# A hybrid pool, DeltaNet and latent-attention block: instruction order from a different scheduling model

## The chip, the cores and the metric

The kernel runs on one core of one Trainium2 chip. Times are device microseconds of one launch. The kernel before has a median of 1241.43 us over three runs (1240.97 to 1242.66). Its profiled execution took 1246.92 us, 5.5 us above that median, of which 1245.1 us is the span from the first to the last instruction.

## The reference

One block over 1024 tokens of width 1024, in float32. All three mixers read one projection of the normed input, and an MLP follows:

```python
h = rms_norm(x, attn_norm[l])
proj = h @ w_in[l]
xa, qkv, z, b, a, c_q, c_kv, k_pe = jnp.split(proj, offsets, axis=-1)
y_a = pool_mixer(xa, ...); y_b = gated_deltanet(qkv, z, b, a, ...); y_c = mla_attention(c_q, c_kv, k_pe, ...)
x = x + jnp.concatenate([y_a, y_b, y_c], axis=-1) @ w_out[l]
h = rms_norm(x, mlp_norm[l])
x = x + jnp.square(jax.nn.relu(h @ w_up[l])) @ w_down[l]
```

The part that matters here is the DeltaNet recurrence. For each of 4 heads a 128 x 128 state passes through the tokens in chunks (64 in the reference, 128 in the kernel), each step of which needs the state of the step before:

```python
v_new = u_i - w_i @ state
o = qd_i @ state + at_i @ v_new
state = state * gl_i + kd_i.T @ v_new
```

## The kernel before

Matrix products in float32 are made of three matmuls on split operands (`mm3`, lines 122 to 125, and `prod`, line 1164 on). A projection tile of 128 columns (`proj_tile`, line 479) is two halves of 512 tokens, and each half is 24 such matmuls into one PSUM bank of tag `mm`. There are 18 tiles: keys, gates, queries, values and the pool mixer.

The stages, in the order of time of the profile:

- 0 to 31 us: loads, norm and transposes of x, then the small projection group (`group`).
- 31 to 168 us: key projections, convolution and SiLU on VectorE and ScalarE (`conv_silu`), key products (line 558), and the latents of attention (`latents`), a queue of generator steps that `pump` advances after each half tile.
- 168 to 222.5 us: `lanes` (line 576 on), the inverses of 32 small triangles, on VectorE, from a DRAM copy of the key products. Their result returns through DRAM (`t_dram`) and feeds `levels` (line 714 on), small 64-row matmuls at line 751.
- 222.5 to 415 us: `chain(h)` for the four heads, 8 chunks each. A chunk is a closed circle between TensorE and VectorE: lines 793 and 794 (state times keys and queries), 796 on VectorE, 801, 805 on VectorE, 810, 815 on VectorE, and then 793 of the next chunk:

```python
PE.matmul(pks[:, 0:P], kt[:, cs_], st, start=True, stop=True)
V.scalar_tensor_tensor(rr, pks[:, 0:P], neg_eg[:, c, h:h + 1], vs[:, c, :], op0=ALU.mult, op1=ALU.add)
PE.matmul(pv_[:, 0:P], tt2[:, c, :], rr, start=True, stop=True)
V.tensor_scalar(vd, pv_[:, 0:P], kd[:, h, c:c + 1], None, op0=ALU.mult)
PE.matmul(pss[:, 0:P], kk[:, c, :], vd, start=True, stop=True)
V.scalar_tensor_tensor(ns, st, el[:, c, h:h + 1], pss[:, 0:P], op0=ALU.mult, op1=ALU.add)
```

  After each four chunks the outputs are normed on VectorE (lines 828 to 832) and transposed on TensorE (line 836). Queries, values, gates and mixer tiles are projected in the same stretch, with `side.append(chain(h))` and `pump` deciding in the source how many chain steps follow each half tile.
- 415 to 530 us: attention (`scores`, `piece`, `weighted`).
- 530 to 720 us: the output product (`out_tile`, with `mm3`), the second norm (`stats`, `spread` with line 1138), and the first MLP products.
- 720 us to the end: the MLP in Strassen-like products (lines 1168 and 1402).

What sets the order on each engine is the framework. The source is traced in program order; a scheduler then simulates the program with a timing model and lets each engine issue what that model says is ready, in order of priority, which follows the program order (`tc.high_priority` lifts `lanes`, and `tc.manual_schedule` keeps the first SyncE loads as written). The list that comes out is fixed: at run time every engine executes its own list in that order, and an instruction that waits holds back all that stand behind it on its engine.

## Time and profile before

| | |
|---|---|
| median of three runs | 1241.43 us |
| profiled execution | 1246.92 us, span 1245.1 us |
| TensorE busy | 1177.1 us, 95% |
| VectorE busy | 858.9 us, 69% |
| ScalarE busy | 570.5 us, 46% |
| GpSimd busy | 292.1 us, 23% |
| chain that ended last | TensorE 72%, VectorE 12%, GpSimd 4%, DMA 4%, ScalarE 4%, issue 3% |

Busy time counts an instruction from its start to its modelled end. TensorE's matmuls overlap each other, so a stretch in which it is always busy isn't a stretch at its peak rate; what such a stretch lacks is idle time. The granted clock is given as a share of full speed: 1.00 is 2.4 GHz and 0.50 is 1.2 GHz.

### The profile page before, as it was taken

The numbers are of one execution on the slowest core, as the hardware profiler recorded it, in microseconds if no ns is written. First come the engines' busy times: TensorE is split into PE (matmuls) and PEld (weight loads), VectorE is DVE, ScalarE is ACT, GpSimd is POOL, SyncE is SP. The second block draws the span as 40 slices with busy tenths as digits, with TensorE's granted clock in tenths as the row PEclk, the third lists the DMA queues.
The fourth block names the chain that finished last, engine by engine and source line by source line (L and its number), as shares of the span: only waits on it lengthen the run. The fifth ranks groups of instructions, "written<-read, shape, count | busy, mean of one in ns | idle before, by whom it ended". The sixth has DMA issues, their size and how long they took to land.

```text
span 1245.1 us, 16313 instructions
## 1 busy us (share of the span) xinstructions
PE 1177.1 (95%) x5802; PEld 966.1 (78%) x5802; DVE 858.9 (69%) x1547; ACT 570.5 (46%) x1187; POOL 292.1 (23%) x327
## 2 busy tenths in 40 slices
PE   6999997899999879998999999999999999999998
PEld 5967775688777658786887788888888888888887
DVE  7576659576576548833688776676659897786863
ACT  6554531455353448722355454555554433333330
POOL 0135542110111285424304334243220000000000
PEclk9999999798999969998999999999999999999999
DMA  7202331211101130184123434433469964442202
GB/s 255 66 19 75 132 104 57 48 50 29 35 14 45 57 106 18 35 330 161 43 77 135 169 144 161 161 144 144 159 228 341 372 220 158 152 136 101 94 26 101
DMA packets 85697, 152.61 MB, mean 123 GB/s; under 512 B 25456, under 2 KB 28656, under 8 KB 85616
## 3 DMA queue, kind: packets, MB, share of 16 engines
q1 hardware_dynamic: 76624, 144.23, 32.9%
q10 hardware_dynamic: 8992, 7.34, 1.9%
q8 instruction: 46, 0.75, 0.2%
q14 instruction: 35, 0.29, 0.1%
HBM read 105.41 MB, written 46.14 MB: 122 GB/s over the span
## 4 chain that ended last, share of the span: by engine, by line
PE 72%; DVE 12%; POOL 4%; DMA 4%; ACT 4%; issue 3%; SPq 0%; POOLq 0%; DVEq 0%; ACTq 0%
PE mm L1402 14%; PE mm L1168 12%; PE sm L1168 6%; PE ch L1402 5%; PE sm L1402 5%; PE mm L125 4%; PE mm L124 4%; PE mm L123 4%; PE ch L1168 3%; DMA upr<-in_w_up_dram 2%; PE sm L751 2%; PE ch L125 1%; DVE tl L588 1%; PE ch L123 1%; PE ch L124 1%
## 5 line engine op out<-in xcount | busy, mean ns | idle before, releaser
L1402 PE MATMUL mm<-dop,dop 128*128 128x512 f32 x768 | 176.0, 389 | 0.0
L1402 PEld LDWEIGHTS mm<-dop,dop 128*128 128x128 f32 x768 | 144.1, 188 | 29.9
L1168 PE MATMUL mm<-H,wop 128*128 128x512 f32 x576 | 139.2, 394 | 3.0 <-DVE uo L1233 3.0
L1168 PEld LDWEIGHTS mm<-H,wop 128*128 128x128 f32 x576 | 108.9, 190 | 27.1 <-DVE uo L1233 4.0
L115 ACT CAST dop<-wdr 128x1024 fp32r<-128x1024 f32 x48 | 50.4, 1050 | 152.5 <-PE mm L1402 62.9
L123 PE MATMUL mm<-H,w 128*128 128x512 f32 x280 | 116.3, 415 | 0.2 <-DVE zs L710 0.2
L125 PE MATMUL mm<-H,w 128*128 128x512 f32 x280 | 115.2, 411 | 0.0
L124 PE MATMUL mm<-H,w 128*128 128x512 f32 x280 | 114.3, 408 | 0.0
L1168 PE MATMUL sm<-op,wop 128*128 128x512 f32 x384 | 92.4, 389 | 1.4 <-ACT p L1231 1.4
L116 POOL TENSOR_TENSOR w<-raw,w 128x1024 fp32r<-128x1024 f32 x15 | 36.5, 2433 | 221.9 <-ACT w L115 191.7
L1168 PEld LDWEIGHTS sm<-op,wop 128*128 128x128 f32 x384 | 72.0, 188 | 16.8 <-ACT p L1231 1.9
L116 DVE TENSOR_TENSOR dop<-wdr,dop 128x1024 fp32r<-128x1024 f32 x48 | 58.6, 1221 | 31.1 <-ACT dop L115 31.1
L1255 ACT ACTIVATE uo<-uo 128x512 f32<-128x512 f32 x48 | 30.3, 631 | 96.9 <-DVE uo L1233 57.0
L116 DVE TENSOR_TENSOR wop<-s,wop 128x512 fp32r<-128x512 f32 x64 | 44.1, 704 | 38.4 <-ACT wop L115 38.4
L1402 PE MATMUL sm<-dop,dop 128*128 128x512 f32 x288 | 67.4, 389 | 0.0
L1402 PE MATMUL ch<-dop,dop 128*128 128x512 f32 x288 | 67.4, 389 | 0.0
L116 DVE TENSOR_TENSOR dop<-H,dop 128x1024 fp32r<-128x1024 f32 x52 | 63.2, 1215 | 0.0
L1402 PEld LDWEIGHTS ch<-dop,dop 128*128 128x128 f32 x288 | 54.1, 188 | 11.2
L1402 PEld LDWEIGHTS sm<-dop,dop 128*128 128x128 f32 x288 | 54.0, 188 | 11.2
L502 DVE SCALAR_TENSOR_TENSOR t2k<-mm,cw,t2k 128x511 f32<-128x511 f32 (+2 forms) x72 | 53.4, 742 | 11.7 <-ACT t2k L499 11.4
L1205 POOL TENSOR_TENSOR s<-upr 128x512 f32<-128x512 f32 x16 | 24.1, 1504 | 159.2 <-DVE uo L1194 73.5
L125 PEld LDWEIGHTS mm<-H,w 128*128 128x128 f32 x280 | 54.0, 193 | 9.1
(395 smaller groups left out, 2684.5 us busy)
## 6 DMA issues: line engine op xcount, KB each, us to landing
H<-u_dram SPq DMA_DIRECT2D x52, 512.0 KB, 4.3
upr<-in_w_up_dram SPq DMA_DIRECT2D x38, 512.0 KB, 4.0
u_dram<-t SPq DMA_DIRECT2D x64, 256.0 KB, 2.0
wdr<-in_w_down_dram SPq DMA_DIRECT2D x32, 512.0 KB, 7.7
u_dram<-uo SPq DMA_DIRECT2D x48, 256.0 KB, 2.1
raw<-in_w_tiles_dram SPq DMA_DIRECT2D x18, 512.0 KB, 3.5
wor<-in_w_out_dram SPq DMA_DIRECT2D x10, 512.0 KB, 8.9
x<-in_x_dram SPq DMA_DIRECT2D x8, 512.0 KB, 3.5
```

Of the source, the lines that this page charges most:

```text
L115: A.copy(hi, src)
L116: (eng or V).tensor_tensor(lo, src, f32(hi), op=ALU.subtract)
L123: PE.matmul(o, ah, bh, start=first, stop=False)
L124: PE.matmul(o, ah, bl, start=False, stop=False)
L125: PE.matmul(o, al, bh, start=False, stop=last)
L502: V.scalar_tensor_tensor(acc[:, s:], pm[:, :512 - s], w, acc[:, s:], op0=ALU.mult, op1=ALU.add)
L588: V.tensor_tensor(TL[:, j + 1:32, 0:m], TL[:, j + 1:32, 0:m], tv, op=ALU.subtract)
L751: PE.matmul(pa[:, c, :], lhs[:, c, :], rhs[:, c, :], start=True, stop=True)
L1168: PE.matmul(o, x_, y_, start=(first and j == 0 and q == 0), stop=(j == 3 and q == 2), skip_group_check=True)
L1205: G.tensor_tensor(v.s12[:, 0], a21, a22, op=ALU.add)
L1255: A.activation(o, o, AF.Relu)
L1402: PE.matmul(o, x_[:, cs_], y_, start=(q in (0, 1, 3) and i == 0 and e == 0), stop=(i == GP - 1 and e == 2), skip_group_check=True)
```

## The change

One argument of the framework's context is set, so that its scheduler takes the timeline simulator for its timing model in place of the default one. The instructions, their sizes, the tiles and the number of buffers are the same; only the order on the engines (and the waits that this order needs) is another.

```diff
-    with tile.TileContext(nc) as tc:
+    with tile.TileContext(nc, schedule_with_timeline_sim=True) as tc:
         block_kernel(tc, *args, o)
```

The order moves on all engines, most of all in the stretch of the key projections and the four chains. On TensorE, in the circle of the second head (`ch` is the PSUM bank of the chain, `mm` that of a projection, `st`, `rr`, `vd` and `vh` what VectorE and ScalarE make between the chain's matmuls), before:

```order
L793 MATMUL ch_600_3166<-st_597_3159,kt_146_982 128x128
L794 MATMUL ch_600_3166<-st_597_3159,qt_369_2294 128x128
L123 MATMUL mm_680_3448<-H_3_99,w_630_3251 128x512
L124 MATMUL mm_680_3448<-H_5_101,w_630_3251 128x512
L125 MATMUL mm_680_3448<-H_3_99,w_631_3252 128x512
L801 MATMUL ch_603_3173<-rr_601_3169,tt2_412_2446 128x128
L123 MATMUL mm_680_3448<-H_3_99,w_630_3251 128x512
L124 MATMUL mm_680_3448<-H_5_101,w_630_3251 128x512
L125 MATMUL mm_680_3448<-H_3_99,w_631_3252 128x512
L810 MATMUL ch_606_3179<-vd_605_3176,ktok_409_2433 128x128
L817 MATMUL ch_608_3183<-vh_604_3175,E_81_691 128x128
L123 MATMUL mm_680_3448<-H_3_99,w_630_3251 128x512
```

and now:

```order
L793 MATMUL ch_600_3166<-st_597_3159,kt_146_982 128x128
L794 MATMUL ch_600_3166<-st_597_3159,qt_369_2294 128x128
L801 MATMUL ch_603_3173<-rr_601_3169,tt2_412_2446 128x128
L810 MATMUL ch_606_3179<-vd_605_3176,ktok_409_2433 128x128
L817 MATMUL ch_608_3183<-vh_604_3175,E_81_691 128x128
L793 MATMUL ch_610_3188<-st_607_3181,kt_146_982 128x128
L794 MATMUL ch_610_3188<-st_607_3181,qt_369_2294 128x128
```

The projection matmuls (lines 123 to 125) that stood two or three between each two steps of the circle stand elsewhere; the steps follow each other directly.

On TensorE at the end of that head and the start of the next (line 836 transposes the normed output `lv`; line 801 is the next head's first chunk), before, with 14 projection matmuls of `mm_718` in the row, of which the first two are shown:

```order
L817 MATMUL ch_615_3199<-vh_614_3197,E_81_691 128x128
L123 MATMUL mm_718_3593<-H_2_98,w_678_3444 128x512
L124 MATMUL mm_718_3593<-H_4_100,w_678_3444 128x512
...
L836 MATMUL ch_642_3340<-ident_79,lv_569_3053 128x128
L801 MATMUL ch_650_3383<-vs_581_3077,tt2_550_2975 128x128
L836 MATMUL ch_642_3340<-ident_79,lv_569_3053 128x128 x3
L125 MATMUL mm_718_3593<-H_2_98,w_679_3445 128x512
```

and now:

```order
L801 MATMUL ch_613_3195<-rr_611_3191,tt2_412_2446 128x128
L817 MATMUL ch_615_3199<-vh_614_3197,E_81_691 128x128
L836 MATMUL ch_642_3340<-ident_79,lv_569_3053 128x128
L801 MATMUL ch_650_3383<-vs_581_3077,tt2_550_2975 128x128
L836 MATMUL ch_642_3340<-ident_79,lv_569_3053 128x128 x3
L810 MATMUL ch_653_3389<-vd_652_3386,ktok_547_2962 128x128
L817 MATMUL ch_655_3393<-vh_651_3385,E_86_704 128x128
L123 MATMUL mm_792_3945<-H_2_98,w_784_3894 128x512
```

The transposes of line 836 now follow the head's last chain matmul at once, and the rest of the next head's first chunk follows them; the projection in that place was issued earlier.

On TensorE at the second norm (line 1138 spreads the norm's factors over the partitions; `mm_1158` and `mm_1160` are tiles of the output product), before:

```order
L124 MATMUL mm_1158_5874<-y_982_4718,H_1124_5562 128x512
L125 MATMUL mm_1158_5874<-y_982_4718,H_1124_5562 128x512
L123 MATMUL mm_1158_5874<-y_506_2818,H_1124_5562 128x512
L1138 MATMUL ch_1154_5851<-dg_1153_5849,ones_86 128x512
L1138 MATMUL ch_1154_5851<-dg_1153_5849,ones_86 128x512
L124 MATMUL mm_1158_5874<-y_506_2818,H_1124_5562 128x512
L125 MATMUL mm_1158_5874<-y_506_2818,H_1124_5562 128x512
L123 MATMUL mm_1158_5874<-y_644_3347,H_1124_5562 128x512
```

and now:

```order
L123 MATMUL mm_1160_5916<-y_961_4625,H_1124_5562 128x512
L124 MATMUL mm_1160_5916<-y_961_4625,H_1124_5562 128x512
L125 MATMUL mm_1160_5916<-y_961_4625,H_1124_5562 128x512
L123 MATMUL mm_1160_5916<-y_982_4718,H_1124_5562 128x512
L124 MATMUL mm_1160_5916<-y_982_4718,H_1124_5562 128x512
L1138 MATMUL ch_1154_5851<-dg_1153_5849,ones_86 128x512
L125 MATMUL mm_1160_5916<-y_982_4718,H_1124_5562 128x512
L123 MATMUL mm_1160_5916<-y_506_2818,H_1124_5562 128x512
```

The product of line 1138 stands 22 output matmuls later: 17 of `mm_1158` and 5 of `mm_1160` went ahead of it.

## Rows read from the trace of the kernel before

**Rows 1.** Span and mean granted TensorE clock of the core.

```profile
core 0: 1245.1 us, clock 0.971
```

**Rows 2.** Busy time by stage: columns as the first row names them, last three clock, DMA.

```profile
core 0: us, PE busy (x) PEld busy (x) DVE busy (x) ACT busy (x) POOL busy (x), PEclk, DMA share, GB/s
31.00:168.00 137.00, 132.65 (x665) 109.21 (x663) 90.67 (x275) 70.09 (x210) 50.55 (x94) 1.00 0.22 72
168.00:222.50 54.50, 39.73 (x176) 32.31 (x177) 42.12 (x99) 9.74 (x15) 21.04 (x32) 0.91 0.29 97
222.50:415.00 192.50, 183.14 (x1175) 148.69 (x1175) 124.30 (x377) 89.39 (x295) 23.03 (x17) 0.93 0.12 30
415.00:470.00 55.00, 43.37 (x212) 33.05 (x213) 28.52 (x48) 28.38 (x65) 32.37 (x39) 0.78 0.30 102
530.00:600.00 70.00, 63.97 (x281) 51.91 (x280) 30.52 (x52) 22.17 (x34) 24.48 (x18) 0.95 0.62 220
720.00:1245.10 525.10, 521.45 (x2301) 431.46 (x2299) 379.12 (x417) 222.87 (x314) 66.70 (x41) 1.00 0.47 168
```

**Rows 3.** Who TensorE waited for: total us, times, longest us.

```profile
...
PE sm L751 <- DMA lv<-t_dram: 13.9, 1, 13.9
...
PE ch L1138 <- DVE dg L1136: 5.8, 1, 5.8
PE s L926 <- ACT H L937: 4.9, 1, 4.9
...
PE ch L836 <- DVE lv L832: 3.7, 2, 2.3
PE ch L836 <- DMA lv<-t_dram: 3.0, 1, 3.0
```

**Rows 4.** Timeline of one chunk: start, us, engine, line, operation, tiles, [idle before].

```profile
...
319.07 0.39 PE L793 MATMUL ch<-st,kt 128*128 128x128 f32 x2
...
319.44 0.47 PE L123 MATMUL mm<-H,w 128*128 128x512 f32 x1
...
319.72 0.35 DVE L796 SCALAR_TENSOR_TENSOR rr<-ch,neg_eg,vs 128x128 f32<-128x128 f32 x1 [0.61 <-PE ch L794]
319.75 0.39 PE L124 MATMUL mm<-H,w 128*128 128x512 f32 x1
...
319.98 0.40 PE L125 MATMUL mm<-H,w 128*128 128x512 f32 x1
...
320.22 0.40 PE L801 MATMUL ch<-rr,tt 128*128 128x128 f32 x2
...
320.65 0.35 DVE L805 TENSOR_SCALAR vd<-ch,kd 128x128 f32<-128x128 f32 x1 [0.58 <-PE ch L801]
...
321.15 0.46 PE L810 MATMUL ch<-vd,ktok 128*128 128x128 f32 x2
...
322.16 0.39 PE L793 MATMUL ch<-st,kt 128*128 128x128 f32 x2
```

**Rows 5.** Timeline at the end of a head, the last one.

```profile
...
410.97 0.49 PE L817 MATMUL ch<-vh,E 128*128 128x128 f32 x2
...
414.68 0.88 DVE L832 TENSOR_SCALAR lv<-lv,sr 128x128 f32<-128x128 f32 x4
...
415.02 0.72 PE L836 MATMUL ch<-ident,lv 128*128 128x128 f32 x3
```

**Rows 6.** Stretches with the lower granted clock (column PEclk).

```profile
213.00:233.40 20.40, 10.44 (x73) 9.32 (x74) 11.07 (x26) 5.53 (x11) 0.00 (x0) 0.50 0.35 88
294.90:305.10 10.20, 10.20 (x58) 8.68 (x58) 4.19 (x11) 4.50 (x18) 0.00 (x0) 0.50 0.10 38
438.30:458.70 20.40, 12.87 (x36) 9.07 (x37) 6.49 (x12) 7.97 (x20) 20.19 (x28) 0.50 0.28 94
```

**Rows 7.** Timeline, TensorE: fourth head's first key transposes and its last key products.

```profile
146.85 0.60 PE L520 MATMUL sm<-ident,kt 128*128 128x128 f32 x4
...
164.03 1.16 PE L558 MATMUL sm<-kt 128*128 128x128 f32 x8
```

## The prediction

> **What bounds the kernel now.** I read the span and the clock first: 1245.1 us at a mean granted clock of 0.971 [rows 1]. Then busy time by stage, to see where TensorE is the limit. From 720 us on it is busy for 521.45 of 525.1 us: nothing can be won there by order, and its list in that part is nearly the old one. In the chains' stage (222.5 to 415) it is busy for 183.14 of 192.5 us at a clock of 0.93, so the stage has 9.36 us idle. In 168 to 222.5 it idles 14.8 us, in 415 to 470 11.6 us at a clock of 0.78 [rows 2]. Then who TensorE waited for: one wait of 13.9 us at line 751 for the inverses from DRAM, 5.8 at line 1138, 4.9 at line 926, 6.7 in three waits at line 836 [rows 3]. So the kernel is bound by TensorE's work, with a few single waits, and the question of this change is where an order puts the independent matmuls (projections) that fill the waits of the dependent ones.
>
> What one chunk of a chain costs shows in the timeline [rows 4]. Line 793 starts at 319.07, line 801 at 320.22, line 810 at 321.15, the next 793 at 322.16: steps of 1.15, 0.93 and 1.01 us, 3.09 together. The steps hold three, three and two projection matmuls (the order of before shows this chunk), which follow each other every 0.23 us (319.75 to 319.98): 8 x 0.23 = 1.86 us. The rest, 3.09 - 1.86 = 1.2 us, is TensorE's own share of the chunk. VectorE's three operations each wait for the matmul before them and are waited for by the next (line 796 starts 0.61 us after its last predecessor on VectorE and waits for 794; line 805 likewise for 801). The circle is one of latency, and the projections ride in it free.
>
> **The change, part by part.** It adds and removes no operation, so every cost is a filler that is gone or a wait that is filled. All sums are made against the profiled 1246.92 us, which is 5.5 us above the median of 1241.43; the difference found is then put on the median.
>
> (a) Bare steps. In the four heads there are 87 steps between dependent matmuls (793 to 801, 801 to 810, 810 to 793). In the list before, none is without something else between; in the list now 42 are bare, in four stretches: the second half of the first head into the second, the second half of the second (its piece is shown), the second half of the third, and nearly all of the fourth. The fillers stand in clumps instead: 13 steps with 13 or more projections hold 237 of them, where before 7 such steps held 132. A clump is longer than the step it covers, so the surplus covers nothing. A bare step keeps its latency, and TensorE idles for the 1.86 / 3 = 0.62 us that fillers took: 42 x 0.6 = +25 us. Bounds: if a step shrinks by one interval of 0.23 us, since the returning matmul no longer stands behind a filler, 42 x 0.39 = +16; if it keeps all of it, 42 x 0.62 = +26. I take +25, by the latencies of the row, because VectorE's two waits show no slack in it.
>
> (b) The norm at the end of four chunks. Line 817 starts at 410.97; the transposes of the normed output (line 836) can start when line 832 has made it, at 415.02 [rows 5]: 4.05 us, of which 0.23 is line 817's own issue, so 3.8 us of idling where nothing stands between. Now 836 follows 817 directly in six of the eight places (one is shown), and the first 801 of the next head's chain stands behind it, so the next chain can't cover it. One of the six has some small products ahead of it, about 2 us by their count. 6 x 3.8 - 2 = 21, less the 6.7 us that TensorE already waits there [rows 3] = +14. Low bound +7: if three of the six are late already for another reason, 3 x 3.8 + 2.3 - 6.7. High bound +14, as all idle time is counted.
>
> (c) The clock. It fell to 0.50 after the long wait (213.0 to 233.4: busy 10.44 of 20.40 us), and from 438.3 to 458.7, where TensorE was busy 12.87 of 20.40; it was also at 0.50 from 294.9 to 305.1 although busy for all of it [rows 6]. So thin work goes with the lower level, and the level can last some 10 us into full work. A bare chunk is busy 1.2 of 3.09 us, thinner than either of the first two. Bounds: 0, if it stays at the present mean of 0.93; above, 14 bare chunks (42 / 3) with 1.1 us more each at half rate = 15.6, and behind each of four stretches 10.2 us at half rate, which lose 5.1 each, 20.4; less what the stage already loses, 0.07 x 192.5 = 13.5: +22.5. The nearest rows lie on both sides, and I take +8, somewhat below the middle, since the bare stretches are short.
>
> The Trainium skill, in "TensorE: Matmul & The Clock Gate", Part 1, section "What's actually happening", says that throttled is the default and that activity releases it. By that alone the clumps behind each stretch would run at the full level, and (c) would be 15.6 - 13.5 = +2; the stretch at 294.9, busy throughout and still at 0.50, speaks against so quick a release, and by it (c) is +22.5. The trace agrees with the rule only in that thin work came with the lower level.
>
> (d) 31 to 168 us. Projections are drawn ahead here: the fourth head's key transposes and products (line 520 at 146.85 to line 558 at 164.03, about 18.3 us with the last product [rows 7]) held 45 projection matmuls, 45 x 0.23 = 10.4 us, that are now issued earlier, so this dependent tail runs almost bare. Line 558 feeds `lanes` through DRAM, and `lanes` feeds the 13.9 us wait; the same seven tile halves as before stand ahead of line 751. What is late here is late there. Bounds: the stage's whole idle time, 137.0 - 132.65 = 4.35 us, won [rows 2]; 10.4 lost. I take +4, nearer to the loss, since the products start after the fillers.
>
> (e) Line 1138. 22 output matmuls, 22 x 0.23 = 5.1 us, now go ahead of it, so its wait of 5.8 us is filled: -5. Bounds: -6.0, all the idle time of 530 to 600 (70 - 63.97 us [rows 2]), and 0 if the second norm's consumers, which start 5 us later, are late instead.
>
> (f) 415 to 470. The first score blocks move up into the fourth chain, ahead of the mixer tile's 24 matmuls (5.6 us), which can now lie where line 926 waited 4.9 us. Bounds: -11.6, all idle of the stage, and +3. I take -3, because line 926 still waits for ScalarE's H.
>
> (g) The other queues. SyncE issues the late weights in another order at 900 to 1000 us, and some output matmuls move into attention's tail. I cost these at nothing: TensorE's row after 720 is full, and that work hides them. If a weight came late the cover would be gone, with a loss of its lateness; the stage's DMA share of 0.47 [rows 2] leaves room.
>
> Sum: 25 + 14 + 8 + 4 - 5 - 3 = +43. Profiled 1246.92 + 43 = 1290; on the median 1241.43 + 43 = **1284 us**. Its own range takes (a) and (b) low with (c) at 2 and the rest as taken, 16 + 7 + 2 + 4 - 5 - 3 = +21, and (c) at its top, +57.5: 1262 to 1299.
>
> **Rivals.**
> 1. *The gains outweigh (faster).* The mechanism is the idle and the slow clock of 415 to 470: if the early score blocks and the mixer's matmuls close it, 11.6 us of idling go, and the 0.22 x 55 = 12 us at half rate; with line 1138 (6.0) and the 4.35 us of (d) that is -34. It decides where it exceeds (a) and (b) at their low bounds, 16 + 7 = 23: -11, or 1230. For it: the stage has 24 us to give. Against: its wait for H stays, and the clock there fell with a wait that isn't TensorE's to fill. 8%.
> 2. *Order makes no difference.* Bare steps would have to be paid back exactly, since TensorE's total work is fixed: the clumps taken earlier leave less to do at the end. That holds only where the clumps lie over idle time; the stage has 9.36 us of it and the bare steps need 25. Within 2.5 us, 1241. 4%.
> 3. *A smaller loss.* The circle shrinks to +16, the norm waits cost +7, the clock holds, (d) is 0, (e) -6, (f) -5: +12, or 1253. For it: VectorE and ScalarE are less pressed when no convolution competes with the chain. 14%.
> 4. *The clock stays low.* (c) at +22.5, (d) at +10.4, and the gains of (e) and (f) lost to the lower rate: 25 + 14 + 22.5 + 10.4 = +72, or 1313. For it: the stretch from 294.9. Against: the clumps are 13 or more matmuls long and dense. 20%.
>
> **How the numbers follow.** Forecast 54%, smaller loss 14%, clock 20%, no difference 4%, faster 8%. A measurement of this kernel tells a change from none at about 0.2%, 2.5 us. Slower 54 + 14 + 20 = 88%, same 4%, faster 8%. The range leaves out the faster case and no difference (12%) and some of the highest: 1250 to 1318.
>
> **What would show it.** In the profile after: TensorE's idle time in the chains' stage rises from 9 to some 45 us, with waits at 801, 810 and 793 for VectorE's `rr`, `vd` and `st` that hardly show now (a), and six waits of 3 to 4 us at 836 (b). The mean clock falls below 0.971 (c). Line 751 starts after 222.5 by some 4 us (d). The wait at 1138 is gone (e), that at 926 shorter (f), and from the MLP on the length is the old one within 3 us (g). I am wrong if the waits at 801, 810 and 793 stay in the order of 10 us in total, or if the stage before 222.5 or the one after 415 changes by more than 15 us.

## The result, and the profile after

The changed kernel takes 1359.74 us (median of four runs, 1357.02 to 1362.82) beside 1242.05 us for the kernel before: a ratio of 1.0934, 95% interval 1.0904 to 1.0965. It is slower by 117.7 us, where 43 was forecast, and lies above the stated range of 1250 to 1318. The sign was right; the size was not, and behind the chains, where a gain was forecast, there is a loss.

The span and the granted clock, which answer to [rows 1]:

```profile
core 0: 1355.3 us, clock 0.936
```

The order is the only change, so the two traces can be cut at the same events: the last key product (line 558), the first matmul of line 751, the last transpose of line 836, the first of line 1128 and the last output matmul. Here is TensorE by these cuts, first of the kernel before (it is [rows 2] cut elsewhere):

```profile
core 0: us, PE busy (x), PEclk, DMA share, GB/s
31.00:165.20 134.20, 130.34 (x656) 1.00 0.21 70
165.20:222.50 57.30, 42.04 (x186) 0.92 0.30 101
222.50:416.10 193.60, 184.22 (x1181) 0.93 0.12 30
416.10:573.60 157.50, 143.56 (x798) 0.92 0.36 125
573.60:622.40 48.80, 42.77 (x189) 0.93 0.21 73
622.40:1245.10 622.70, 614.63 (x2707) 1.00 0.45 161
```

and of the changed kernel:

```profile
33.00:189.40 156.40, 140.45 (x668) 0.92 0.20 67
189.40:243.40 54.00, 40.82 (x177) 0.93 0.27 87
243.40:514.10 270.70, 225.93 (x1257) 0.81 0.10 26
514.10:677.70 163.60, 131.62 (x721) 0.90 0.32 114
677.70:721.60 43.90, 42.25 (x190) 1.00 0.22 78
721.60:1355.30 633.70, 618.00 (x2705) 0.99 0.45 158
```

Row by row the difference is +22.2, -3.3, +77.1, +6.1, -4.9 and +11.0 us, and +2.0 before the first cut: 110.2, the difference of the spans (the execution profiled before lies 4.9 us above its median, that of the changed kernel 2.7 below). The chains' stage also does 76 matmuls more than before (1257 against 1181), and the next row 77 fewer, so some of its 77 us is work drawn ahead from the row of +6.1. TensorE is idle for 44.8 us in it (270.70 - 225.93), as forecast (45), but the row is longer by 77: idle time alone doesn't price it.

Who TensorE waited for, which answers to [rows 3] (total us, times, longest us):

```profile
PE ch L836 <- DVE lv L832: 17.6, 5, 3.5
PE mm L123 <- ACT H L115: 11.6, 2, 11.4
...
PE ch L801 <- DVE rr L796: 8.2, 16, 1.8
PE sm L520 <- DVE kt L510: 8.1, 2, 5.5
...
PE s L926 <- ACT pr L937: 7.5, 1, 7.5
PE ch L810 <- DVE vd L805: 7.1, 13, 1.0
```

The waits of the chain's circle that the prediction named are there (801, 810, 836), and the wait at 1138 is gone. The wait at 926, forecast to shrink from 4.9 us, has grown to 7.5. The waits at lines 520 and 123 were not forecast.

The circle of [rows 4] without its fillers, in the third head (TensorE; start, us):

```profile
441.43 0.49 PE L801 MATMUL ch<-rr,tt 128*128 128x128 f32 x2
442.37 0.49 PE L810 MATMUL ch<-vd,ktok 128*128 128x128 f32 x2 [0.44 <-DVE vd L805]
443.38 0.49 PE L793 MATMUL ch<-st,kt 128*128 128x128 f32 x2 [0.23 <-DVE st L815]
444.53 0.49 PE L801 MATMUL ch<-rr,tt 128*128 128x128 f32 x2 [0.44 <-DVE rr L796]
...
447.61 0.80 PE L801 MATMUL ch<-rr,tt 128*128 128x128 f32 x2 [0.44 <-DVE rr L796]
...
451.81 0.80 PE L801 MATMUL ch<-rr,tt 128*128 128x128 f32 x2 [0.44 <-DVE rr L796]
```

and the clock over the same time:

```profile
440.40:447.00 6.60, 4.74 (x29) 1.00 0.11 32
447.10:465.80 18.70, 11.95 (x36) 0.54 0.07 21
```

From 801 to 801 the first two chunks take 3.10 and 3.08 us at the full clock: what a chunk with eight projection matmuls in it took before. The next takes 4.20, when the clock has fallen: the single matmul (two records of 128 columns) lasts 0.80 instead of 0.49 us. The clock is at 0.50 for some time in each of the four bare stretches (from 324.3, 382.4, 447.2 and 484.8 us on), 88.8 us together. So the fillers were free, as the prediction had it, and a bare chunk pays for the lower clock too. The busy time in such a stretch is no measure of work: a lone matmul is busy for all of its 0.39 to 0.80 us, one in a row for 0.23.

The end of a head, which answers to [rows 5] (TensorE's wait ahead of its transposes):

```profile
506.99 0.47 PE L836 MATMUL ch<-ident,lv 128*128 128x128 f32 x1 [3.51 <-DVE lv L832]
```

The 3.8 us of step (b) are 3.51 here.

Each chain matmul can be matched with its own in the other trace. Over the 87 steps of the four heads (first chain step to last) TensorE has about 154 us of issue time in both kernels, an estimate from the distance of matmuls in full rows; the steps take 172.9 us before and 232.6 after. The 42 bare steps take 55.7 us after and hold 16.0 of issue; 12 steps with the transposes of 836 take 68.3 and hold 33.8; the rest 108.6 and 104.1. Before, the steps with 836 lost 9.1 us and all others 10.1. Part of the fillers now stands ahead of the first chain step, where 72 projection matmuls lie instead of 14: from line 751 to that step it takes 25.5 us instead of 14.7.

### The profile page after: what moved, and what is told of

Read it like the earlier page. It is cut to its first block, busy times and chain, and to the rows that moved or that the text cites. A ratio compares the mean times of both kernels' runs of the same rounds, so it can differ in the third digit from the quotient of the medians.

```text
span 1355.3 us, 16329 instructions
## 1 busy us (share of the span) xinstructions
PE 1219.4 (90%) x5802; PEld 1001.4 (74%) x5802; DVE 856.8 (63%) x1547; ACT 574.7 (42%) x1187; POOL 292.2 (22%) x327
## 5 line engine op out<-in xcount | busy, mean ns | idle before, releaser
L123 PEld LDWEIGHTS mm<-H,w 128*128 128x128 f32 x280 | 55.4, 198 | 15.7 <-issue 2.8
L123 PE MATMUL mm<-y,H 128*128 128x512 f32 x128 | 50.9, 405 | 14.8 <-ACT H L115 11.6
L124 PEld LDWEIGHTS mm<-H,w 128*128 128x128 f32 x280 | 55.4, 198 | 11.3 <-issue 0.7
L125 PEld LDWEIGHTS mm<-H,w 128*128 128x128 f32 x280 | 54.9, 196 | 11.9 <-issue 0.7
L1402 PEld LDWEIGHTS sm<-dop,dop 128*128 128x128 f32 x288 | 54.1, 188 | 11.2
## 6 DMA issues: line engine op xcount, KB each, us to landing
wor<-in_w_out_dram SPq DMA_DIRECT2D x10, 512.0 KB, 11.4
```

What stands on the lines that cost most here:

```text
L123: PE.matmul(o, ah, bh, start=first, stop=False)
L124: PE.matmul(o, ah, bl, start=False, stop=False)
L125: PE.matmul(o, al, bh, start=False, stop=last)
L1402: PE.matmul(o, x_[:, cs_], y_, start=(q in (0, 1, 3) and i == 0 and e == 0), stop=(i == GP - 1 and e == 2), skip_group_check=True)
```

## The experiments

Each experiment is one of the two programs with the issue order of some engines held fixed by order-only edges between neighbours (`set_order`, after the program is traced). Nothing else changes unless the diff says so; the diffs are shortened, with the lists given by name. `OLD` and `NEW` are the lists of the two kernels; `a | b` stands for list a up to an event, then list b for what is left. Each has two timings (before_warm751 ten, before_1138 twelve) beside the kernel before on the same chip; the chips differ between groups of runs, so ratios are compared.

**Which engine's order: pe_after and pe_before_tl.**

```diff
+        set_order(tc, PE=NEW)      # pe_after: the others by the default model
+        set_order(tc, PE=OLD)      # pe_before_tl: the others by the timeline simulator
```

> TensorE's list is that of the changed kernel, held fixed; the other engines are ordered by the default model around it. Theory A (TensorE's order alone makes the loss, by bare chain steps and the lower clock behind them): 1330 to 1365 us, granted clock 0.93 to 0.94, TensorE idle 120 to 140 us. Theory B (the orders of VectorE, ScalarE and the DMA queues make it, TensorE only shows the waits): under 1290 us, clock over 0.955.

> The opposite: TensorE's list is that of the kernel before, held fixed, and all other engines are ordered by the timeline simulator. Theory A: 1240 to 1265 us, clock about 0.97. Theory B: over 1300 us.

Measured: 1378.77 us, ratio 1.1071 (1.1025 to 1.1116), clock 0.919; and 1280.29 us, 1.028 (1.0225 to 1.0335), clock 0.968. TensorE's list is the larger part, and theory B falls. But pe_after is above its range, and pe_before_tl too: letting the timeline simulator order the other engines costs 35 us around the old list of TensorE, and saves some 17 around the new one (1.1071 against 1.0934). So the price of one engine's order depends on the orders of the others.

**Which stage: early_after, chain_after, late_after, mlp_after.**

```diff
+        set_order(tc, all=NEW until L751 | OLD)              # early_after
+        set_order(tc, all=OLD until L751 | NEW until end of chains | OLD)   # chain_after
+        set_order(tc, all=OLD until end of chains | NEW)     # late_after
+        set_order(tc, all=OLD until end of output product | NEW)            # mlp_after
```

> All engines follow the changed order up to the first small matmuls at line 751 (243.4 us of its profile) and the old order from there on. In the profiles that point comes 20.9 us later than before. Theory A (losses of the stages add up): 1263 us (1256 to 1270). Rival C (what is late there is made up by work that was drawn ahead): under 1250.

> All engines follow the old order up to line 751, the changed order from there to the end of the four chains, and the old order after them. Theory A: the stage takes 270 us as in the changed kernel, +77, so 1319 us (1305 to 1330), with TensorE's clock near 0.81 in that stage. Rival C (the chains are slow because keys, inverses and convolutions come late from the stage ahead): under 1285.

> The old order on all engines to the end of the four chains, the changed order from there on. The stages measured so far (start to line 751: +18, chains: +67) leave some 30 us of the whole loss for this part; theory A as predicted gave this part a gain of 8. If the part is slow by itself (new waits at the score blocks, at line 879 and of 11.4 us at the output product): 1262 to 1280. If it is slow only because of what the chains left it (work drawn ahead, clock low on entry): 1235 to 1255.

> The old order on all engines to the end of the output product (622.5 us of the profile before), the changed order from there on. If the MLP is slower by its own order (its two halves take 5.3 and 5.7 us more in the changed kernel's profile): 1252 to 1258. If it was slow only because of what it followed: 1241 to 1248.

Measured: 1263.65 us, ratio 1.0146 (1.0093 to 1.0200); 1312.24, 1.0536 (1.0485 to 1.0588); 1278.09, 1.0264 (1.0216 to 1.0313); 1260.45, 1.0125 (1.0087 to 1.0163). In us against the kernel before beside them: +18.3, +66.9, +31.5 and, as a part of the last, +16.1. The first three sum to 116.7 (each with some 6 us either way), the whole loss is 117.7. So the stages add up within the noise: no large part of what is late in one is made up in the next, and the chains lose as much behind the old start as behind the new one (rival C of both expectations falls). The surprise is the last part: 31.5 us by itself. By the cuts used above its first and last row are

```profile
414.10:597.00 182.90, 149.70 (x799) 0.87 0.31 109
642.70:1276.00 633.30, 617.70 (x2705) 0.99 0.45 158
```

against 157.5 and 622.7 before: +25.4 between the chains and the second norm, and +10.6 in the MLP (-3.1 between the two), whose order had been costed at nothing. The +16.1 of mlp_after has an interval of 10.8 to 20.3; its own trace has the MLP 11.8 us longer, the changed kernel's 11.0. So the MLP is about a third of this part.

In chain_after the stage shows as in the changed kernel:

```profile
223.70:497.30 273.60, 228.71 (x1257) 0.80 0.10 26
```

It is 80.0 us longer than before and the kernel 66.9, so some 13 us of it is work drawn ahead and given back later. In the changed kernel's own rows the same work makes the chains' row look dearer and the row of +6.1 cheaper than the runs of single stages do.

**What the clock costs in the chains: fill_bare, fill_all, fill_po.** Matmuls that nothing needs are put into TensorE's waits, on top of the new order; one of the places is shown.

```diff
+                warm((h, c, 801), pv_[:, 2 * P:3 * P], kt[:, cs_])
                 PE.matmul(pv_[:, 0:P], tt2[:, c, :], rr, start=True, stop=True)
+        set_order(tc, all=NEW)
```

> The changed order on all engines, held fixed, with two more matmuls (128x128, keys times keys into unread columns of the chain's own bank) ahead of the second matmul of each of the 42 bare steps: 84 matmuls of work that nothing needs, in TensorE's idle time. Theory A with the clock (thin stretches put TensorE at half rate, and that costs some 40 us of the chains' stage): the added work makes the kernel faster, 1320 to 1345 us, granted clock of the chains' stage up from 0.81 to 0.88 or more. Rival (the lower clock is there whatever stands in these steps, or costs nothing since the steps are latency): 1358 to 1385 us, clock in the stage unchanged.

> As the run before, and also 12 such matmuls ahead of the transposes of the normed output (line 836 of the changed kernel) in seven of the eight places, where TensorE waits 3.5 us. Theory A with the clock: 1300 to 1330 us, the stage's clock 0.93 or more, no waits at 836 over 1.5 us. Rival: 1355 to 1390.

> As fill_all, but the added matmuls go into unread columns of the chain bank that was filled last instead of the one to be filled next (in fill_bare they waited for that bank and put some 0.4 us into each circle: a chunk takes 3.47 us there, 4.20 in the changed kernel, 3.08 in the kernel before). 84 in the bare steps, 12 each ahead of the transposes in the five places where TensorE waits 3.5 us. If the lower clock is what makes a bare chunk 4.20 instead of 3.08: chunks of 3.08 to 3.2 us at a clock of 1.00, and 1335 to 1348 us, 12 to 20 less than the changed kernel. If it is the missing overlap itself: chunks stay over 3.5 and the time within 5 us of fill_all's 1353.

Measured: 1361.62 us, ratio 1.0935 (1.0882 to 1.0988); 1353.69, 1.0872 (1.0821 to 1.0923); 1374.10, 1.1035 (1.0990 to 1.1079). None gains what the theory with the clock wanted, and fill_po is outside both of its forecasts; fill_all is 6 us below the changed kernel, with intervals that overlap. The reason is not that the clock stayed low. In fill_bare it is 0.88 over the chains' stage, and in fill_all it is nearly full:

```profile
243.00:504.00 261.00, 240.16 (x1588) 0.97 0.11 28
```

The stage, from its first matmul at line 751 to its last transpose, is still some 261 us instead of 270.7. The added work lengthens the circle it was to fill. In fill_bare (line 778 is the added work; 808, 818 and 799 are 801, 810 and 793 of the other programs):

```profile
446.14 0.47 PE L818 MATMUL ch<-vd,ktok 128*128 128x128 f32 x2
447.06 0.52 PEld L778 LDWEIGHTS ch<-kt 128*128 128x128 f32 x4 [0.34 <-DVE st L823]
447.06 0.71 PE L778 MATMUL ch<-kt 128*128 128x128 f32 x4
447.61 0.39 PE L799 MATMUL ch<-st,kt 128*128 128x128 f32 x2
```

The added work starts only at 447.06, when VectorE has read the bank it writes, and the state's matmul follows it at 447.61: 1.47 us after 818, where the bare step at the full clock (442.37 to 443.38) takes 1.01. A chunk takes 3.47 us there. In fill_po, with the added work in the bank filled last, VectorE waits for that work, and a chunk takes 3.97. Work that shares the circle's banks is no free filler; the projections before had banks of their own. These runs show that the low clock is not the bulk of the loss: 0.97 instead of 0.81 goes with a stage 10 us shorter, of 77. The added work itself lengthens a bare chunk from 3.08 to 3.47; for 14 chunks that is 5.5 us, so a full clock without it would give back some 15, by this estimate.

**Is the long wait what lowers the clock? before_warm751.** The old order, with 56 such matmuls in the wait of 13.9 us (first head only).

```diff
+            for _ in range(56):
+                PE.matmul(pw[:, 3 * P:4 * P], KT[0][:, 0:P], KT[0][:, 0:P], start=True, stop=True)
         pa = bat(64, 32, a_pair, t_even)
```

> The order of the kernel before, held fixed, with 56 matmuls that nothing needs (keys times keys, 128x128, some 12 us) in TensorE's wait of 13.9 us ahead of line 751. Theory A with the clock: TensorE comes out of the wait at 1.00 instead of 0.50 for the 12 us behind it, a gain of 4 to 7 us, 1236 to 1241. Rival (the clock fell for another reason, or the chains' start is latency): no difference, within 2 us.

Measured: 1247.31 us, ratio 0.9999 (0.9973 to 1.0026): the rival. The windows of the wait and of what follows it:

```profile
210.00:222.60 12.60, 11.10 (x100) 1.00 0.38 113
222.70:234.60 11.90, 11.20 (x84) 0.57 0.21 32
```

The wait is filled and the clock is at 1.00 in it. Before, it fell 4.4 us into the wait, at 213.0. Now it falls at 224.2, when line 751 has begun, and stays at its lower level to 234.5, in a stretch where TensorE is busy for 11.2 of 11.9 us. So the wait was not what the low level behind it needed, as my reading of [rows 6] had it: the lower level inside the wait cost nothing, and the one behind it comes without the wait too.

**The early stage: early_510y.**

```diff
+        kt = C((P, 1024), "kt", 2) if h > 1 else U(s="kt")
+        set_order(tc, all=NEW until L751 | OLD, with L510 of heads 3 and 4 behind their L502 on VectorE)
```

> early_after (changed order to line 751, old order from there; 1263.7 us, +18) with the last step of the key convolutions of heads 3 and 4 (line 510, four operations on VectorE) right behind the sums of line 502 they belong to, instead of behind the norm of the latents (lines 325 to 134) and the key products of the head before (line 561); the key tiles of these two heads get buffers of their own, since in the shared ring they wait for a latent tile to be released. If VectorE's order makes the stage late: TensorE's waits at line 520 (9.2 and 6.1 us) shrink, and 1250 to 1258. If TensorE's order does (projections ahead of the latents): within 3 us of 1263.7.

What it rests on, VectorE and TensorE in the changed kernel: the key tile of the fourth head is finished by the operation at 172.97, behind the key products of the third (line 561) and the norm of the latents; TensorE waits for it.

```profile
172.71 0.34 DVE L561 SCALAR_TENSOR_TENSOR at<-sm,c,E 128x128 f32<-128x128 f32 x1
172.97 0.68 DVE L510 SCALAR_TENSOR_TENSOR kt<-t2k,t2k 128x512 f32<-128x512 f32 x1
```

```profile
173.70 0.69 PE L520 MATMUL sm<-ident,kt 128*128 128x128 f32 x2 [5.46 <-DVE kt L510]
```

Measured: 1259.83 us, ratio 1.0117 (1.0069 to 1.0165), beside 1.0146 (1.0093 to 1.0200): the intervals overlap, so this is inconclusive (in the profiles line 751 starts at 239.5 instead of 243.4 us). The waits at 520 for the key tile are gone from its profile, and in their place stand five, 10.9 us, at the same line behind line 561. One queue's order is not the cause by itself. What both traces do show is what moved: projections were drawn ahead (the half tile of 132.8 to 142.8 us before ends at 127.3 now), the matmuls of the latents, the first few aside, fall behind by 16 to 35 us, and the fourth head's key transposes by 27 (146.85 to 173.70). That the one makes the other late is read from the traces; no run isolates it.

**The late weights: late_wor, late_wor2, late_mm.**

```diff
+        set_order(tc, late_after's lists, with on SP: L1094 (wor_1125, wor_1126) ahead of the first L1106)     # late_wor
+        set_order(tc, late_wor's lists, with on ACT: L115 (H_1124) behind the second group of loads of L1263)  # late_wor2
+        set_order(tc, late_after's lists, with on PE: 72 output matmuls behind the last L974)                  # late_mm
```

> late_after (old order to the end of the chains, changed order from there; 1278.1 us) with one edit on SyncE: the two loads of the second piece of the output weights (line 1094) are issued ahead of the store of the first output tile (line 1106), behind which they stand in the changed kernel. If that store holds the loads back until the first output tile is done, and so makes the wait of 10.3 us at line 123: the wait goes, 1266 to 1271. If the loads are late because of bandwidth or because their cast stands behind other work on ScalarE: within 3 us of 1278.

> late_wor with the two casts of those weights on ScalarE moved ahead of the loads and squares of the output tiles (lines 1263 and 1116) behind which they stand. In late_wor the loads are issued 50 us earlier and TensorE still waits 6.9 us, for the cast. If ScalarE's list is the second holder: that wait under 2 us, 1264 to 1271. If not: within 3 us of late_wor's 1276.

> late_after (1278.1 us) with the 72 output matmuls of TensorE's list that stand among the last transposes and products of attention (lines 957 to 974) put behind the last of these. If they hold up the tail of attention, and with it the last two of its outputs, which all four open output tiles wait for: attention ends some 15 us earlier and the kernel takes 1264 to 1272. If they only fill waits there: 1276 to 1290.

The wait in the changed kernel, of 11.4 us, as SyncE's and ScalarE's queues show it (`wor` is the second piece of the output weights, SPq and ACTq the issue of a DMA):

```profile
636.98 0.33 SPq L1106 DMA_DIRECT2D x_dram<-x  x1
...
637.36 0.90 SPq L1094 DMA_DIRECT2D wor<-in_w_out_dram  x2
...
647.86 1.04 ACT L115 CAST H<-wor 128x1024 fp32r<-128x1024 f32 x1 [8.08 <-DMA wor<-in_w_out_dram]
```

The loads stand behind the store of the first output tile, on SyncE, in both lists, and in both traces that store comes some 6.5 us behind the last matmul of attention (533.8 and 637.0 us). What differs is the work left to cover the loads. Before, the first tile ends while TensorE still has output matmuls of the others to do; now the four open tiles end within 2 us of each other, and almost nothing is left:

```profile
533.80:549.00 15.20, 15.20 (x69) 1.00 0.98 361
637.00:648.90 11.90, 0.58 (x3) 0.70 0.95 353
```

Measured: late_wor 1275.94 us, ratio 1.0246 (1.0204 to 1.0289, beside late_after's 1.0264). The loads are issued at 501.9 us there, and the wait is still 6.92 us, since the cast stands behind loads that wait, on ScalarE:

```profile
561.15 1.04 ACT L115 CAST H<-wor 128x1024 fp32r<-128x1024 f32 x1 [4.29 <-DMA x<-in_x_t_dram]
```

late_wor2 takes this away too: 1272.39 us, 1.0221 (1.0184 to 1.0258); the wait at 123 is gone, and one of 4.1 us at line 125 for VectorE's half of the same weights has come. late_mm: 1275.13 us, 1.0243 (1.0205 to 1.0281). There attention does end 16.5 us earlier (549.7 to 533.2), but the open tiles still end together: the first is stored at 554.4, when their matmuls are all but done, the loads follow it, and the wait at 123 is still 9.9 us. Each of the three runs is lower than late_after, by 2 to 5 us, with intervals that overlap; none gives what its theory wanted. Of the 25 us that the row behind the chains costs, the two holders of the weights account for about 5, by runs whose intervals overlap. TensorE's waits in that row sum to 33 us in late_after and to 13 before; beside the 10.3 at line 123 those at 926 (7.2) and 879 (3.7) are the longest. What makes them wasn't tried.

In the MLP the trace shows single waits at stage borders (mlp_after, TensorE), and with two of these, of 2.4 and 2.7 us, the lower clock (from 651.8 to 658.6 and from 969.3 to 976.1 us):

```profile
PE mm L1402 <- DVE H L1407: 2.7, 1, 2.7
PE mm L1168 <- DVE uo L1233: 2.6, 2, 1.8
PE mm L1323 <- ACT op L115: 2.4, 1, 2.4
```

With its other waits they sum to 9.9 us, where the kernel before waits 4.4 in the MLP. In the changed kernel the waits there sum to 11.9, so 7.5 of the 11.0 us of its MLP are waits. Which instruction's place makes them wasn't tried.

**Step (e) alone: before_1138.** The old order, with one matmul moved on TensorE.

```diff
+        set_order(tc, all=OLD, with on PE: the first L1138 behind 22 more output matmuls)
```

> The order of the kernel before, held fixed, with the first product of line 1138 moved on TensorE behind the 22 output matmuls that stand ahead of it in the changed kernel. By step (e) of the prediction the wait of 5.8 us goes: 1237 to 1240 beside 1242 to 1246, 3 to 5 us faster. If what needs the second norm is then late: no difference.

Measured: 1239.72 us, ratio 0.9969 (0.9951 to 0.9987), over 12 runs. The wait falls from 5.8 us to 0.6, and the stretch of 573.6 to 622.4, 48.8 us before, takes 43.1. This version beats the kernel before, by 0.3%.

## Why the prediction was right in its sign and wrong in its size

**The sign and the main place: right.** TensorE's work is fixed, and the new order takes projections out of the waits of a latency-bound circle. That fillers were free shows in the bare chunk of 3.08 us at the full clock, the same as the filled one. A sign of being wrong that the prediction set itself has come all the same: the stage before line 751 changed by more than 15 us (+20.9). And the MLP, which was to keep its length within 3 us, took 11.0 more.

**(a), bare steps, +25: right, its companion apart.** 42 steps take 55.7 us with 16.0 of issue. At 3.08 us for three steps they would take 43.1, a loss of 27. Of the other 12.6, some 10 lie in the 24 bare steps that ran wholly at 0.50; the rest is in a few long steps at the full clock.

**(b), transposes behind the norm, +14: too small.** The single wait was right (3.51 beside 3.8 us), and five of them, not six, sum to 17.6. But the steps that hold the transposes lose 34.5 us now and 9.1 before, +25: I had counted the wait alone and not the lone matmuls on either side of it, the chain's next link among them.

**(c), the clock, +8: the mechanism right, the size too small, and my reason for [rows 6] wrong.** The clock fell in each of the four bare stretches, and added work kept it up. In bare steps it costs the 10 us above, where the upper bound had 15.6 (14 times 1.1 is 15.4); over the whole stage fill_all gives back 10 us, or some 15 by the estimate there. My measure was wrong: a bare chunk is not busy for 1.2 of 3.09 us, as its issue time is, but for about 70% (4.74 of 6.60 us at the full clock), more than the rows that I compared it with. The rival with the clock at its top is not what happened: its time of 1313 was passed for other reasons. That the low level behind the long wait needs that wait is refuted by before_warm751.

Together (a) to (c) were +47, and chain_after measures 66.9.

**(d), the first 168 us, +4: the direction right, mis-sized.** early_after measures +18.3, above the upper bound of 10.4. I had priced the projections drawn ahead as a delay of what stands behind them on TensorE, once. By the traces the delay runs on through VectorE and ScalarE to the next head: latents late by 16 us and more, keys behind them. That path is argued, not shown; early_510y settled nothing.

**(e), line 1138, -5: right.** before_1138 shows it alone, and the row of 573.6 to 622.4 is 4.9 us shorter in the changed kernel.

**(f) and (g), -3 and nothing: this failed, and it is the largest part of the miss.** From the end of the chains on I forecast -8 with (e), and late_after measures +31.5. For (f) I counted the one wait at 926 as filled. It grew instead, from 4.9 to 7.2 us, and the row from the chains to the second norm is 25.4 us longer in late_after: one part of it is that the open output tiles end together and leave almost nothing to cover the loads of the output weights (10.3 us at line 123, a wait that no term of mine held). For (g) the step that failed is the one that read TensorE's full row after 720 us as proof that order there costs nothing: full, it had no time to win, but all to lose, and it loses 11 us, most of it in new waits. The same row was to cover SyncE's loads, but the loads that came late are those of 534 us, ahead of it, behind a store whose time I had not followed. Most of the 25.4 us has no cause shown.

By the runs of single stages the miss of 75 us is thus some 20 in the chains, 14 at the start and 40 behind the chains.

## What to carry to other kernels

A list that is well filled has much to lose and little to gain from another order: price each stage for what its fillers hide, the full ones first, and follow each moved load to the store or the cast that stands ahead of it on its queue. The orders of the engines are one plan: TensorE's new list among lists made by the default model was slower than both kernels (1.1071), and its old list among lists made by the timeline simulator slower than the kernel before (1.028). Where one matmul waits, moving that one matmul was worth more than a new plan for all.

## What was not expected of the hardware

In before_warm751 TensorE's clock went to its lower level soon after 12.6 us at 1.00 of 128x128 matmuls, in a stretch where the engine was busy for 11.2 of 11.9 us:

```profile
222.94 1.09 PE L751 MATMUL sm<-lv,w 64*64 64x32 f32 x16 [1.84 <-issue]
224.20:234.50 10.30, 10.02 (x66) 0.50 0.18 28
```

Ahead of the fall stand a gap of 1.84 us and the first small matmuls of line 751. The level then lasted through ten projection matmuls in a row (most of them 0.63 us long, where one takes 0.39 at the full clock). So a high busy share of a row does not tell that the clock was full. Whether the gap or the small matmuls brought it down, no run separates.
